# New tokens' values and outputs between rows and columns: DMA transfers of single elements through memory in place of PE transposes, in a RetNet/HGRN2 decoder step

## The chip, the cores and the metric

The kernel runs on one core of one Trainium2 chip. The metric is the device time of one launch in microseconds (us). All times of the trace come from one profiled execution and are counted from the start of its span.

The engines are named as the profile names them: PE (matrix multiply; PEld is its weight load), DVE (vector), ACT (scalar and activation), POOL, and SP, which only issues DMAs here. A name with q (SPq) is an engine's instruction queue. DMAs can also be issued from ACT and POOL; they stand in that engine's own order of instructions.

## The reference

One decoder layer for 512 prompt tokens and 8 new tokens, of width 1024, in fp32. After a norm, one wide product gives the inputs of two branches.

```python
z = h @ w_in                                   # rq rk rv rg gq gf gi gg a_ret a_hg
o_r, s_ret = retention_chunked(q_r, k_r, v_r, log_gamma, s_ret0)     # 4 heads, 128 x 256 states
u_r = head_norm_gate(o_r, ret_norm_g, rg) @ w_up_ret
o_g, s_hg = gla_chunked(q_g, k_g, v_g, log_f, s_hg0)                 # 8 heads, 128 x 128 states
u_g = head_norm_gate(o_g, hg_norm_g, gg) @ w_up_hg
m = sigmoid(a_ret) * u_r + sigmoid(a_hg) * u_g
r = r + m @ w_o
r = r + square(relu(rms_norm(r) @ w_ff1)) @ w_ff2
r = r + sigmoid(rms_norm(r) @ w_ple_gate) * (p_l @ w_ple_proj)
```

The change concerns the 8 new tokens of both branches. For each token `b` and head, with its own state `S`:

```python
S = decay * S + outer(k, v)      # decay: one number per head (retention) or one per key channel (HGRN2)
o = q @ S                        # then normed over the head's values and gated
```

The outputs are the layer's results for the prompt and the new tokens and all updated states.

## The kernel before

**Layout.** Activations lie by channel: 128 channels on the partitions, the `N = 520` tokens (512 prompt, 8 new) along the free dimension, in `T:N` the new ones. A product with 128 columns of weights is a *unit*: its weights `raw` are loaded by SP (`load`, L142; 128 rows of a weight's 128 columns per partition, 8 blocks), cut into a high and a low part (`prep`, L199: ACT writes `wh` at L221, DVE `wl` at L226), and multiplied in three passes of 8 blocks and two halves of the tokens (`mm`, L239: 48 matmuls at L243). The result is in one of two pairs of psum banks (`pm`); an evacuation by ACT or DVE takes it out. Other matmuls and transposes use four single banks (`bank`).

**Order.** `run_unit` (L269) writes the order out by hand: prepare the weights of a unit two ahead (and issue a load), the first half of the unit's matmuls, then all functions listed in `at[u]`, then the second half, then the evacuation. Engines run their own instructions in that order. The HGRN2 branch has 8 units per pair of heads, for four pairs; retention has 12 units per two heads, twice (L828 to L852). With `b` the first unit of a pair, the HGRN2 steps for new tokens are:

- `b+4` `hg_dec_load` (states loaded as `Sd`, key channels on the partitions), `b+7` `hg_dec_decay` and `hg_vT`,
- `hg_vT` (L468) calls `v_dec` (L453): the 8 new tokens' values, by channel in `vT[:, z, T:N]`, are transposed by PE (L457) into 8 rows of psum, copied by DVE into `vd` (L458) and stored by SP as an 8 x 256 tensor `vdd` in memory (L460). `v_bc` (L463) then loads `vdd` with every row on all partitions, as `vbc`.
- `b+9` and `b+11` `hg_dec_add`: DVE multiplies `vbc` by `k` (L486), adds it to `Sd` (L487), and SP stores the new state.
- `b+12` `hg_dec_out` (L511) calls `o_dec` (L493): four matmuls (L499) of the last 32 tokens' `q` with the state give a 128 x 512 psum block, in which only the rows 24 to 31 of each group of 32 are new tokens, and of each of these rows only the columns of the token's own state count. ACT copies the block to `psd` (L501).
- `b+13` `hg_state` (L528) ends with `o_ext` (L503): four PE transposes of the whole block (L506) and one DVE copy of the entries that count into `odec` (L509), by channel.
- `b+14` `hg_out`: ACT and DVE read `odec` (L565, L568). `b+15` `hg_norm`: `ones_bc` (L584) sums the squares over channels on PE (L590, L591).

Retention, with `o` the first unit of a head's turn (`o` of the second head of two is four units later):

- `o+6` `rt_vT` (L706): loads of `rSd`, PE transposes and ACT copies of the prompt's values (L722), then `v_dec` and two `v_bc`.
- `o+8`, `o+9` `rt_dec_add`: POOL multiplies `vbc` (L755), DVE adds (L756).
- `o+10` `rt_dec_out` (L762): `o_dec`, with `rt["knp"][:, 1]` (in the profile `rkn`) as the block. At the first head of two, `rt_kT` and `rt_vT` of the second head stand in the same unit, behind it.
- `o+11` `rt_ext` (L795), in the middle of the unit: `o_ext`, then the readers of `odec` (ACT L800, DVE L801), the sum of the two squares (DVE L802) and its cut into `rsqH` (ACT L598, DVE L599).
- `o+12` `rt_norm` (L808), in the middle of the unit: `ones_bc` on `rsqH` (PE L590, L591). For the last head it is at the same distance (L1010).

The rest of the layer (the up projections and gates, w_o, the MLP, the gated embedding) follows after about 480 us and is not touched.

Of the kernel before, what the change touches and what calls it, by code (L numbers as in the profile page):

```python
# [8 lines left out]
F32 = mybir.dt.float32  # L9
# [8 lines left out]
T = 512  # L18
NB = 8
N = T + NB  # L20
# [25 lines left out]
def decoder_step_kernel(  # L46
# [27 lines left out]
    V, S, G, PE = nc.vector, nc.scalar, nc.gpsimd, nc.tensor  # L74
    dma = nc.sync.dma_start
# [7 lines left out]
    dp = ctx.enter_context(tc.tile_pool(name="dp", bufs=2, space=DRAM))  # L83
# [11 lines left out]
    vd = cp.tile([8, 256], F32, name="vd")  # L95
    odec = cp.tile([128, 2, 8], F32, name="odec")

    ident = cid[:, C_ID:C_ID + 128]
# [9 lines left out]
    def pair(tag, name, dt=F32):  # L108
        return big.tile([128, 2, N], dt, tag=tag, name=name)

    def bank():
        return pss.tile([128, 512], F32, tag="s", name="s")
# [2 lines left out]
        return ap.rearrange("p (a n) -> p a n", a=2)  # L115

    units = []
    at = defaultdict(list)
    extra = set()
    prep_last = set()  # L120

# [109 lines left out]
    def prep_all():  # L231
        for _ in prep():
            pass
# [5 lines left out]
    def mm(w, k, xh, xl, ps, first, last):  # L239
        wh, wl = w  # L240
        for i, (a, b) in enumerate(((wh, xh), (wh, xl), (wl, xh))):
            for z in range(2):
                PE.matmul(ps[z], lhsT=a[:, k, :], rhs=b[:, z * NH:(z + 1) * NH],  # L243
                          start=first and i == 0, stop=last and i == 2)
# [3 lines left out]
    def run_groups(u, lo, hi):  # L248

        due = []  # L250
        n = 0
        for gi, (slots, start, stop, evac) in enumerate(units[u].groups):
            for si, (k, xs) in enumerate(slots):
                if lo <= n < hi:
                    if si == 0 and start:
                        if gi < 2:
                            t = pm.tile([128, 2, 512], F32, tag="m", name="m")
                            psum_of["cur"] = t[:, :, :NH], [t[:, z, :NH] for z in range(2)]
                        else:
                            psum_of["cur"] = None, [bank()[:, :NH] for z in range(2)]  # L260
                    both, ps = psum_of["cur"]
                    xh, xl = xs()
                    mm(w_of[u], k, xh, xl, ps, start and si == 0, stop and si == len(slots) - 1)
                    if si == len(slots) - 1 and evac is not None:
                        due.append((evac, both if both is not None else ps))
                n += 1
        return due

    def run_unit(u):  # L269
        prep_all()  # L270
        if u in extra:
            prep_all()
        due = run_groups(u, 0, 4)
        for f in at.pop(u, []):
            f()
        for e, ps in due:
            e(ps)
        for e, ps in run_groups(u, 4, 8):
            e(ps)
        w_of.pop(u)  # L280

    def unit(w, c, H, L, evac):
        units.append(Unit(cols(w, c), [([(k, lambda k=k: (H(k), L(k))) for k in range(8)], True, True, evac)]))
# [16 lines left out]
    st = {}  # L300
# [151 lines left out]

    def v_dec(vT):  # L453

        b = bank()
        for z in range(2):
            PE.transpose(b[0:8, z * 128:(z + 1) * 128], vT[:, z, T:N], ident)  # L457
        V.tensor_copy(vd, b[0:8, 0:256])  # L458
        d = dp.tile([8, 256], F32, tag="vd", name="vdd")
        dma(d, vd)  # L460
        return d

    def v_bc(d, z, tag):  # L463
# [29 lines left out]
    def o_dec(q, Sd, psd):  # L493

        b = bank()
        for g in (1, 0):
            for z in range(2):
                i = 2 * g + z
                PE.matmul(b[32 * i:32 * i + 32, :], lhsT=q[g],  # L499
                          rhs=Sd[g][:, 4 * z:4 * z + 4, :], start=True, stop=True)  # L500
        S.activation(psd, b, AF.Copy)  # L501

    def o_ext(psd):  # L503
        b = bank()
        for l in range(4):
            PE.transpose(b[:, l * 128:(l + 1) * 128], psd[:, l * 128:(l + 1) * 128], ident)  # L506

        own = bass.AP(b.tensor, b.offset + 24, [list(b.ap[0]), [64, 2], [36, 2], [129, 4]])
        V.tensor_copy(odec.rearrange("p g (z l) -> p g z l", z=2), own)  # L509

    def hg_dec_out(p):  # L511
        def go():
            q = st["q", p]
            o_dec([q[:, h, N - 32:N] for h in range(2)], [st["Sd", h] for h in range(2)], st["psd"])
        return go

    def hg_kT(p):
# [10 lines left out]
    def hg_state(p):  # L528
        def go():
            kn, vn, tot = st["kn"], st["vn"], st["tot"]  # L530
            Sst = big.tile([128, 2, 4, 128], F32, tag="S11", name="Sst")
            bs = []
            for h in range(2):
                b = bank()
                for c in range(4):
                    PE.matmul(b[:, c * 128:(c + 1) * 128], lhsT=kn[:, h, c, :], rhs=vn[:, h, c, :],  # L536
                              start=True, stop=True)
                bs.append(b)
            for h in range(2):
                V.tensor_copy(Sst[:, h, 0, :], bs[h][:, 0:128])  # L540
            for c in range(1, 4):
                for h in range(2):
                    i = TOFF[128] + c
                    V.scalar_tensor_tensor(Sst[:, h, c, :], in0=Sst[:, h, c - 1, :], scalar=tot[:, h, i:i + 1],
                                           in1=bs[h][:, c * 128:(c + 1) * 128], op0=ALU.mult, op1=ALU.add)
            st["S"] = Sst
            o_ext(st["psd"])
        return go

    def hg_out(p):  # L550
# [46 lines left out]
    def split(H, L, x):  # L597
        S.activation(H, x, AF.Copy)  # L598
        V.tensor_sub(L, x, H)  # L599
# [23 lines left out]
    for p in range(4):  # L623
        b = len(units)
# [22 lines left out]
    rt = {}  # L647
# [48 lines left out]
    def rt_kT(P, e):  # L696
        def go():
            hd = 2 * P + e
            K = rt["K", P][:, e]
            b = bank()  # L700
            for c in range(4):
                PE.transpose(b[:, c * 128:(c + 1) * 128], K[:, c * 128:(c + 1) * 128], ident)
            S.activation(rt["knp"][:, 0, 0:512], b, AF.Copy, scale=cst[:, C_KD + hd:C_KD + hd + 1])
        return go
# [57 lines left out]
    def rt_dec_out(P, e):  # L762
        def go():
            q = rt["Q", P][:, e, N - 32:N]
            o_dec([q, q], [rt["Sd", 0], rt["Sd", 1]], rt["knp"][:, 1, 0:512])
        return go

    def rt_out(P, e):
# [25 lines left out]

    def rt_ext(P, e):  # L795
        def go():
            o_ext(rt["knp"][:, 1, 0:512])
            sq, t = rt["sq"], rt["t"]
            for z in range(2):
                S.activation(sq[:, z, T:N], odec[:, z], AF.Square)  # L800
                V.tensor_tensor(t[:, z, T:N], t[:, z, T:N], odec[:, z], op=ALU.mult)  # L801
            V.tensor_tensor(sq[:, 0], sq[:, 0], sq[:, 1], op=ALU.add)  # L802
            hd = 2 * P + e
            rt["sqH"] = pair(OSLOT[hd], "rsqH", F32R)
            split(rt["sqH"][:, 0], rt["sqH"][:, 1], sq[:, 0])
        return go
# [21 lines left out]
    for P in range(2):  # L828
        b = len(units)
        for e in range(2):  # L830
            unit(W, RK + (2 * P + e) * 128, hk, hl, ev_rope(P, e, "K", KSCALE))
        for e in range(2):
            unit(W, RQ + (2 * P + e) * 128, hk, hl, ev_rope(P, e, "Q", 1.0))
        for e in range(2):
            for base, ev in ((RV, ev_rv), (RG, ev_rg)):
                for z in range(2):
                    unit(W, base + (2 * P + e) * 256 + z * 128, hk, hl, ev(P, e, z))
        for e in range(2):
            o = b + 4 * e
            at[o + 5].append(rt_scores(P, e))  # L840
            at[o + 6].append(rt_kT(P, e))
            at[o + 6].append(rt_vT(P, e))
            at[o + 7].append(rt_state(P, e))
            at[o + 8].append(rt_dec_add(P, e, 0))
            at[o + 9].append(rt_dec_add(P, e, 1))
            at[o + 10].append(rt_dec_out(P, e))
            at[o + 11].append(rt_ext(P, e))
            if P == 0 or e == 0:
                at[o + 12].append(rt_norm(P, e))
                at[o + 12].append(rt_scale(P, e))  # L850
        for e in range(2):
            at[b + 4 * e + 8].append(rt_out(P, e))  # L852
# [568 lines left out]
    for c in range(4):  # L1421
        t = big.tile([128, D], F32, tag=f"S{12 + c}", name=f"xn{c}")
# [172 lines left out]
    for u in flow[2:]:  # L1595
        if isinstance(u, int):
            run_unit(u)
        else:
            run_pair(*u)
# [68 lines left out]
```

## Time and profile before

| | us |
|---|---|
| median of 3 runs | 1088.88 |
| the three runs | 1087.69, 1088.88, 1089.11 |
| the profiled execution | 1087.63 |
| its span | 1085.8 |

TensorE's mean granted clock in the profiled execution is 0.999. The span is what the engines' instructions cover; the execution's own time is 1.83 us longer. In a timeline row stand the start, the length, the engine, the line, the operation and `output<-input`, with `x` and the number of instructions merged into the row, and in brackets the time for which the engine was idle before it and what it waited for. The length of a matmul includes its way through the array; matmuls in a row overlap. Names in the profile are those of the program's tiles: `vT` and `rvT` are the values by channel, `cid` holds the identity, `s` is any single psum bank, `m` a pair of them.

### The profile page before, as it was taken

The page shows a single profiled execution, that of the slowest core. Times are in us where ns is not written, and L with a number is a line of the kernel's source. Part 1 is how long each engine was busy: PE and PEld are TensorE (multiplying, and loading weights), DVE is VectorE, ACT ScalarE, POOL GpSimd, SP SyncE. Part 2 cuts the span into 40 slices and gives each one's busy share as a digit, 9 for nine tenths or more (in the row PEclk, how much of TensorE's full clock was granted, in tenths as well). Part 3 has the DMA queues.
Part 4 walks back from the last instruction along what each step waited for, and adds up shares of the span by engine and source line. Part 5 has one row for each costly group of instructions (what it writes and reads, how often), then busy time and mean ns, then how long its engine had stood idle before and what let it go on. Part 6 is the DMA issues. An engine that isn't in the chain of part 4 may idle for free.

```text
span 1085.8 us, 23533 instructions
## 1 busy us (share of the span) xinstructions
PE 1074.4 (99%) x10197; PEld 1057.2 (97%) x10197; DVE 686.2 (63%) x1074; ACT 508.6 (47%) x853; POOL 103.8 (10%) x95
## 2 busy tenths in 40 slices
PE   8999999999999999999999999999999999999997
PEld 8999999999999999999999999999999999999997
DVE  6576676858754844775666656855555555554565
ACT  7323534334254333554444345545455445544556
POOL 1000000000011010112222000011211211100001
PEclk9999999999999999999999999999999999999999
DMA  7556253442456355437778532355566566544302
GB/s 224 156 178 176 84 150 91 137 123 86 130 162 177 105 156 169 134 96 174 187 179 189 149 98 81 95 123 150 142 151 156 148 155 145 137 117 117 98 20 80
DMA packets 234952, 147.23 MB, mean 136 GB/s; under 512 B 5320, under 2 KB 229840, under 8 KB 234592
## 3 DMA queue, kind: packets, MB, share of 16 engines
q1 hardware_dynamic: 211600, 125.54, 39.1%
q0 software_dynamic: 23104, 19.93, 10.4%
q8 instruction: 80, 1.31, 0.5%
q14 instruction: 24, 0.20, 0.1%
q10 hardware_dynamic: 144, 0.26, 0.1%
HBM read 131.94 MB, written 13.76 MB: 134 GB/s over the span
## 4 chain that ended last, share of the span: by engine, by line
PE 95%; DVE 3%; ACT 1%; DMA 0%; issue 0%; SPq 0%; DVEq 0%
PE m L243 61%; PE s L881 19%; PE m L1394 2%; PE s L1394 2%; PE s L380 1%; PE s L499 1%; PE s L785 1%; PE s L560 1%; PE s L536 1%; PE s L739 1%; PE s L243 1%; PE s L562 0%; PE s L787 0%; DVE wl L226 0%; DVE tmp L659 0%; PE s L363 0%
## 5 line engine op out<-in xcount | busy, mean ns | idle before, releaser
L226 DVE TENSOR_TENSOR wl<-raw,wh 128x1024 fp32r<-128x1024 f32 (+1 forms) x125 | 152.3, 1220 | 69.2 <-ACT wh L221 68.2
L243 PE MATMUL m<-hH,wh 128*128 128x260 f32 x864 | 179.1, 289 | 0.0
L243 PE MATMUL m<-hH,wl 128*128 128x260 f32 x864 | 174.4, 283 | 0.0
L243 PE MATMUL m<-hL,wh 128*128 128x260 f32 x864 | 173.7, 283 | 0.0
L221 ACT ACTIVATE wh<-raw 128x1024 fp32r<-128x1024 f32 (+1 forms) x125 | 130.6, 1047 | 79.8 <-PE m L243 61.9
L243 PEld LDWEIGHTS m<-hH,wh 128*128 128x128 f32 x864 | 132.9, 189 | 2.5 <-issue 0.8
L243 PEld LDWEIGHTS m<-hL,wh 128*128 128x128 f32 x864 | 133.1, 188 | 0.0
L243 PEld LDWEIGHTS m<-hH,wl 128*128 128x128 f32 x864 | 133.1, 188 | 0.0
L881 PE MATMUL s<-comb,wh 128*128 128x260 f32 x672 | 122.1, 282 | 0.0
L881 PEld LDWEIGHTS s<-comb,wh 128*128 128x128 f32 x672 | 103.8, 188 | 0.0
L881 PE MATMUL s<-comb,wl 128*128 128x260 f32 x336 | 95.1, 283 | 0.0
L173 ACT ACTIVATE wh<-cst 128x512 fp32r<-128x512 f32 x80 | 50.3, 628 | 52.7 <-DVE cst L179 27.7
L175 DVE TENSOR_TENSOR wl<-cst,wh 128x512 fp32r<-128x512 f32 x80 | 55.2, 690 | 29.0 <-ACT wh L173 28.4
L243 PE MATMUL m<-fa,wh 128*128 128x260 f32 x384 | 66.9, 283 | 0.0
L243 PE MATMUL m<-oga,wh 128*128 128x260 f32 x384 | 64.6, 283 | 0.0
L881 PEld LDWEIGHTS s<-comb,wl 128*128 128x128 f32 x336 | 63.2, 188 | 0.0
L755 POOL TENSOR_TENSOR vbc<-vbc,K 128x1024 f32<-128x1024 f32 x8 | 17.5, 2198 | 409.4 <-ACT sq L580 298.1
L243 PEld LDWEIGHTS m<-fa,wh 128*128 128x128 f32 x384 | 54.7, 188 | 0.0
L243 PEld LDWEIGHTS m<-oga,wh 128*128 128x128 f32 x384 | 53.7, 188 | 0.8 <-issue 0.8
L1104 DVE TENSOR_TENSOR xT<-xT,m 128x520 f32<-128x520 f32 x32 | 22.3, 696 | 48.4 <-PE m L243 48.4
L243 PE MATMUL m<-fh,wh 128*128 128x260 f32 x256 | 51.5, 282 | 0.0
L243 PE MATMUL m<-fa,wl 128*128 128x260 f32 x256 | 51.5, 283 | 0.0
(396 smaller groups left out, 2438.4 us busy)
## 6 DMA issues: line engine op xcount, KB each, us to landing
raw<-in_w_in_dram SPq DMA_DIRECT2D x56, 512.0 KB, 4.2
raw<-in_w_ff_dram SPq DMA_DIRECT2D x40, 512.0 KB, 4.0
cst<-in_w_ff_dram POOLq DMA_DIRECT2D x48, 256.0 KB, 4.9
rawp<-in_w_ff_dram SPq DMA_DIRECT2D x24, 512.0 KB, 3.6
vbc<-vdd SPq DMA_DIRECT2D x16, 512.0 KB, 4.3
rawp<-in_w_in_dram SPq DMA_DIRECT2D x16, 512.0 KB, 3.4
cst<-in_w_in_dram POOLq DMA_DIRECT2D x28, 256.0 KB, 4.9
Sd<-in_state_hgrn_dram SPq DMA_DIRECT2D x8, 512.0 KB, 5.9
```

The source lines that it names most:

```text
L173: S.activation(wh[:, 4 * h:4 * h + 4], x, AF.Copy)
L175: V.tensor_sub(wl[:, 4 * h:4 * h + 4], x, wh[:, 4 * h:4 * h + 4])
L221: S.activation(wh[:, k], r[:, k], AF.Copy)
L226: e1.tensor_sub(wl[:, k], r[:, k], wh[:, k])
L243: PE.matmul(ps[z], lhsT=a[:, k, :], rhs=b[:, z * NH:(z + 1) * NH], start=first and i == 0, stop=last and i == 2)
L380: PE.matmul(b[32 * j:32 * j + 32, 32 * hc:32 * hc + 32], lhsT=kx[:, h, o:o + 32], rhs=qx[:, h, o:o + 32], start=True, stop=True)
L499: PE.matmul(b[32 * i:32 * i + 32, :], lhsT=q[g], rhs=Sd[g][:, 4 * z:4 * z + 4, :], start=True, stop=True)
L536: PE.matmul(b[:, c * 128:(c + 1) * 128], lhsT=kn[:, h, c, :], rhs=vn[:, h, c, :], start=True, stop=True)
L755: G.tensor_tensor(t, t, rt["K", P][:, e, T:N].unsqueeze(2).to_broadcast([128, 8, 128]), op=ALU.mult)
L881: PE.matmul(out, lhsT=w[:, 4 * half + k, :], rhs=x, start=start and k == 0 and m == 0, stop=k == 3 and m == 2, skip_group_check=not start)
L1104: V.tensor_tensor(h2(xT[:, j]), h2(xT[:, j]), ps, op=ALU.add)
L1394: PE.matmul(ps, lhsT=w[:, k, :], rhs=x, start=k == 0 and n == 0, stop=k == 7 and n == 2)
```

## The change

`v_dec` no longer uses PE, DVE and `vd`: ACT issues two DMAs, each of which writes the 128 channels x 8 tokens of a half of `vT[:, :, T:N]` to `vdd` element by element, with rows and columns exchanged. `o_ext` is replaced by two functions. `o_park` stores the whole 128 x 512 block in memory (`pd`), by a DMA that ACT issues directly behind its copy of the block. `o_fetch` reads the 16 entries per channel that count into `odec`, by four DMAs on SP of 128 x 4 single elements.

For HGRN2, `o_park` stands in `hg_dec_out` (`b+12`) and `o_fetch` where `o_ext` stood (`hg_state`, `b+13`). For retention both stand in `rt_dec_out` (`o+10`). `rt_ext` moves from the middle of unit `o+11` to the end of its matmuls, ahead of its evacuation, by a second list `before_end`.

```diff
@@ run_unit
-        for e, ps in run_groups(u, 4, 8):
+        due = run_groups(u, 4, 8)
+        for f in before_end.pop(u, []):
+            f()
+        for e, ps in due:
             e(ps)
@@ v_dec
-        b = bank()
+        d = dp.tile([8, 256], F32, tag="vd", name="vdd")
         for z in range(2):
-            PE.transpose(b[0:8, z * 128:(z + 1) * 128], vT[:, z, T:N], ident)
-        V.tensor_copy(vd, b[0:8, 0:256])
-        d = dp.tile([8, 256], F32, tag="vd", name="vdd")
-        dma(d, vd)
+            S.dma_start(d[:, z * 128:(z + 1) * 128].rearrange("t v -> v t"), vT[:, z, T:N])
         return d
@@ o_ext becomes o_park and o_fetch
-    def o_ext(psd):
-        b = bank()
-        for l in range(4):
-            PE.transpose(b[:, l * 128:(l + 1) * 128], psd[:, l * 128:(l + 1) * 128], ident)
-
-        own = bass.AP(b.tensor, b.offset + 24, [list(b.ap[0]), [64, 2], [36, 2], [129, 4]])
-        V.tensor_copy(odec.rearrange("p g (z l) -> p g z l", z=2), own)
+    def o_park(psd):
+
+        st["pd"] = dp.tile([128, 512], F32, tag="pd", name="pd")
+        S.dma_start(st["pd"], psd)
+
+    def o_fetch():
+        pd = st["pd"]
+        for i in range(4):
+            g, z = divmod(i, 2)
+            own = bass.AP(pd.tensor, pd.offset + (24 + 64 * g + 36 * z) * 512, [[1, 128], [640, 4]])
+            dma(odec[:, g, 4 * z:4 * z + 4], own)
@@ hg_dec_out
             o_dec([q[:, h, N - 32:N] for h in range(2)], [st["Sd", h] for h in range(2)], st["psd"])
+            o_park(st["psd"])
@@ hg_state
-            o_ext(st["psd"])
+            o_fetch()
@@ rt_dec_out
             o_dec([q, q], [rt["Sd", 0], rt["Sd", 1]], rt["knp"][:, 1, 0:512])
+            o_park(rt["knp"][:, 1, 0:512])
+            o_fetch()
@@ rt_ext
-            o_ext(rt["knp"][:, 1, 0:512])
             sq, t = rt["sq"], rt["t"]
@@ the order of retention
-            at[o + 11].append(rt_ext(P, e))
+            before_end[o + 11].append(rt_ext(P, e))
```

More of the change, by code (lines that the diff above doesn't have):

```diff
@@ L117, in decoder_step_kernel @@
     units = []
-    at = defaultdict(list)
+    at, before_end = defaultdict(list), defaultdict(list)
     extra = set()
```

## The prediction

> **What bounds the kernel now.** The page comes first: busy time by engine, and the chain that ended last.
>
> ```profile
> PE 1074.4 (99%) x10197; PEld 1057.2 (97%) x10197; DVE 686.2 (63%) x1074; ACT 508.6 (47%) x853; POOL 103.8 (10%) x95
> ...
> PE 95%; DVE 3%; ACT 1%; DMA 0%; issue 0%; SPq 0%; DVEq 0%
> ```
>
> PE is busy 99% of the span and makes 95% of the chain. A busy PE need not be at its peak, so the view of who waited for whom, on PE alone, comes next (us in total, times, longest).
>
> ```profile
> PE m L1485 <- DMA xs<-in_x_sample_dram: 3.4, 1, 3.4
> PE s L499 <- DVE Sd L487: 0.9, 1, 0.9
> ...
> ```
>
> It has six rows; the four not shown are under 0.5 us each. The largest lies at the kernel's start. So time taken off PE's stream comes off the span, unless a new wait appears on PE. The question is whether eight times two detours through memory stay behind PE's other work.
>
> **What PE loses.** Each of the eight heads or pairs of heads that are worked on together (four HGRN2 pairs, four retention heads; a "site" below) has two transposes in v_dec (L457) and four in o_ext (L506): 48 in all. Matmuls overlap, so the length of one isn't its price; the step between starts is. PE's timeline in two retention sites (start, length, engine, line; x2 is two instructions merged):
>
> ```profile
> 336.17 0.38 PE L457 MATMUL s<-cid,rvT 128*8 128x128 f32 x2
> 336.31 0.48 PE L243 MATMUL m<-hH,wh 128*128 128x260 f32 x2
> 336.63 0.40 PE L243 MATMUL m<-hL,wh 128*128 128x260 f32 x2
> ...
> 372.20 0.61 PE L506 MATMUL s<-cid,rkn 128*128 128x128 f32 x4
> 372.56 0.49 PE L243 MATMUL m<-hH,wh 128*128 128x260 f32 x2
> 372.89 0.40 PE L243 MATMUL m<-hL,wh 128*128 128x260 f32 x2
> 373.12 0.40 PE L243 MATMUL m<-hH,wl 128*128 128x260 f32 x2
> ```
>
> An undisturbed pair of L243 steps by 0.23 to 0.24 us (372.89 to 373.12). From the first L506 to the second pair behind it is 0.69 us; less one pair, the four cost 0.45 us. From the first L457 to 336.63 is 0.46 us; less one pair, the two cost 0.22 us. Per site that is 0.67 us, for eight **5.4 us**. DVE also loses two copies per site and SP one store; PE waits for neither, so I cost them at nothing.
>
> **What a transfer of single elements costs.** The new v_dec issues, on ACT, two DMAs of 1024 elements of 4 bytes each. o_park stores 256 KB in whole rows. o_fetch issues, on SP, four DMAs of 512 single elements. No row shows a data packet of 4 bytes, so I bound it with these, from the page's DMA parts (packets, MB, share of 16 engines; then issues, KB each, median us to landing):
>
> ```profile
> q1 hardware_dynamic: 211600, 125.54, 39.1%
> ...
> q10 hardware_dynamic: 144, 0.26, 0.1%
> ...
> raw<-in_w_in_dram SPq DMA_DIRECT2D x56, 512.0 KB, 4.2
> ...
> rawp<-in_w_in_dram SPq DMA_DIRECT2D x16, 512.0 KB, 3.4
> ...
> out_dram<-y SPq DMA_DIRECT2D x3, 256.0 KB, 3.0
> ```
>
> q10 is one store of 256 KB, 128 rows of 2 KB, in 144 packets: one per contiguous run and sixteen more. By that rule raw (rows of 128 columns) has 1024 packets of 512 bytes, 64 per engine; rawp (rows of 256) has the same bytes in 512 packets, 32 per engine. It lands 0.8 us sooner, so 32 more packets cost about **25 ns each**: the price of a packet beyond its bytes, which I take for a packet of 4 bytes. The bounds: 0 below (the packets hidden in the fixed part), and 4.2 us over 64, 66 ns, above (raw's whole landing put on its packets). Between them stands the mean of q1: 39.1% of 16 x 1085.8 us over 211600 packets is 32 ns, bytes included.
>
> Both detours thus put 128 packets on each engine: v_dec 2 x 1024 / 16, o_fetch 4 x 512 / 16. At 25 ns that is 3.2 us, with the fixed part on top. SP's timeline prices that one: the broadcast waits for the store of vd, 8 rows.
>
> ```profile
> 67.58 0.30 SPq L460 DMA_DIRECT2D vdd<-vd  x1
> 68.94 0.38 SPq L465 DMA_DIRECT2D vbc<-vdd  x1
> ```
>
> So 1.4 us pass from an issue until the next DMA may read the result, and an issue itself takes 0.30 to 0.38 us.
>
> One rule of the Trainium skill speaks against the change: VectorE: DVE Perf Modes, section The three transpose paths, calls a plain DMA with transposing strides 19 times slower than the crossbar's transpose, for which it gives 1309 ns at 128x128. An estimate from that page: 24.9 us for 16384 elements, 1024 per engine, is 24 ns each, so that rule alone would leave the sum as it is. No run here shows it.
>
> **The values' way (v_dec).** Tightest are the HGRN2 sites after the first. ACT's timeline, then DVE's:
>
> ```profile
> 127.27 1.07 ACT L476 ACTIVATE vn<-s 128x512 f32<-128x512 f32 x2
> ```
>
> ```profile
> 142.02 1.22 DVE L486 TENSOR_TENSOR vbc<-vbc,kx 128x1024 f32<-128x1024 f32 x1
> ```
>
> ACT triggers from 128.3 to 129.1 (2 x 0.38). With 1.4 + 3.2 us the values lie in memory at 133.7; v_bc is issued and lands (0.4 us, and 4.2 us as raw, of its size) at 138.3. DVE wants it at 142.0, so 3.7 us are spare, which last to 53 ns a packet. On SP the weight loads (L237) queue behind the waiting v_bc. In the first site v_bc went at 68.94; now it goes near 70, and a weight is prepared two units ahead of its matmuls (48 matmuls, 24 pairs at 0.24 us, some 6 us a unit), so that does no harm. The triggers hold ACT about 0.8 us; behind them waits an evacuation whose psum buffer PE wants one unit later, and that covers it.
>
> **The outputs' way (o_park, o_fetch).** For HGRN2 there is room: the park is issued at hg_dec_out, the fetch one unit later on SP behind the weight load of 104.12, and its first reader runs at 115.44 on ACT.
>
> ```profile
> 104.12 9.57 SPq L237 DMA_DIRECT2D raw<-in_w_in_dram  x2
> ```
>
> ```profile
> 115.44 0.20 ACT L565 ACTIVATE sq<-odec 128x8 f32<-128x8 f32 x1
> ```
>
> 11.3 us less 1.4 + 3.2: 6.7 us spare. The retention heads decide. Heads 1 and 2 on ACT, on PE (the sums in rt_norm, which must not start late), and on DVE:
>
> ```profile
> 334.94 0.60 ACT L501 ACTIVATE rkn<-s 128x512 f32<-128x512 f32 x1 [2.38 <-PE s L499]
> ...
> 336.09 1.08 ACT L722 ACTIVATE rvn<-s 128x512 f32<-128x512 f32 x2
> ...
> 366.47 0.60 ACT L501 ACTIVATE rkn<-s 128x512 f32<-128x512 f32 x1 [3.10 <-PE s L499]
> ```
>
> ```profile
> 350.10 0.28 PE L590 MATMUL s<-rsqH,ones_r 128*128 128x260 f32 x1
> ...
> 378.40 0.28 PE L590 MATMUL s<-rsqH,ones_r 128*128 128x260 f32 x1
> ```
>
> ```profile
> 373.40 0.17 DVE L509 COPY odec<-s 128x16 f32<-128x16 f32 x1
> ...
> 375.36 0.70 DVE L599 TENSOR_TENSOR rsqH<-rsq,rsqH 128x520 fp32r<-128x520 f32 x1 [0.71 <-ACT rsqH L598]
> ```
>
> From odec present (373.57) to the last input of the sums (376.06) pass 2.5 us. **Head 2:** the park is triggered at 367.1 and lands 3.0 us later (as out_dram<-y, of its size), at 370.2 with the wait; the fetch has until 378.40 - 2.5 - 0.1 = 375.8. That leaves 5.6 us for 1.4 us and 128 packets: enough up to 33 ns each, 1.0 us spare at 25. **Head 1:** the fetch starts at 338.8 and is needed by 347.5, 8.7 us; but v_dec of the next head starts at 337.4 on ACT's queue, so 256 packets per engine share the time and are done at 338.8 + 256 x the price: enough up to 34 ns, 2.3 us spare at 25. Heads 3 and 4 repeat these two. Behind the park's trigger on ACT wait the copies L703 and L722, which PE reads a unit later. While DVE and ACT wait at rt_ext, the evacuation of that unit and the next weight preparation stand behind them; at 25 ns DVE resumes near 375 (370.2 + 4.6), against 373.4, and PE wants that psum buffer only for the unit after next. SP, held by the fetch until the park lands, has state and weight loads behind it, with more than a unit to spare.
>
> **Sum.** The profiled execution took 1087.63 us, 1.83 us more than its span; the median of the runs shown, 1088.88, is 1.25 us above it. 1087.63 - 5.4 = 1082.2 for such an execution, **1083.5 us** as a median, -0.5%.
>
> **Rivals.** Above 34 ns every further ns costs PE 2 x 0.128 + 2 x 0.256 = 0.77 us, so the gain of 5.4 us is gone at 41 ns.
> 1. *A wait on PE takes the transposes' place, about as long*: 37 to 44 ns, 1086.7 to 1091.1, some 1088.5 us. For it: q1's mean of 32 ns lies just below the limit. Against: that mean carries 593 bytes a packet.
> 2. *Slower, by the same mechanism*: the sums of rt_norm wait for o_fetch in all four retention heads, from 41 ns on. At the upper bound of 66 ns it is 32 x 0.77 - 5.4 = +19 us, 1108 us. For it: no row has so small a read or write of memory. Against: the slope of 25 ns from rawp to raw. The Trainium skill, DMA: Bandwidth & Descriptors, section Specifications, says that below 512 bytes the engines read, modify and write; if that doubled the 32 ns, an estimate of 64 ns would land here. No run here shows it.
> 3. *A weight load shares the engines with a fetch*: 64 packets at 32 ns, 2.0 us, of which 1.0 is spare in heads 2 and 4: +2, 1085.5 us. For it: weight loads run throughout. Against: the fetch stands ahead of the next one on SP.
>
> **How the numbers follow.** Forecast 0.50 (own range 1082.3 to 1086.5), rival 1 0.15, rival 2 0.25, rival 3 0.10. Faster by over 0.2% (2.2 us, about what a measurement of this kernel can tell from no change): 0.60; within: 0.15; slower: 0.25. The low end is the forecast less another 1.2 us, the wait of L499 (0.9) and a little more that an unloaded DVE may end. The high end is 53 ns, where the values' way fails too: 1083.5 + 19 x 0.77 = 1098. Beyond the two ends I leave 0.05 and 0.15.
>
> **What would show it.** No L457 and no L506, 48 matmuls fewer, and 8 x 4096 data packets of single elements more. v_dec's DMAs and the fetches landing near 4.6 us where they run alone. No wait of PE at L590 for rsqH, and rt_ext's readers of odec in heads 2 and 4 starting near 8 us after the end of L501. The prediction is wrong if such landings pass 6 us, if PE waits at L590 or for a psum buffer, or if DVE L486 waits for vbc.

## The result, and the profile after

| | before | after |
|---|---|---|
| median of 4 runs, us | 1088.36 | 1105.15 |
| lowest and highest, us | 1087.69, 1089.11 | 1100.73, 1107.81 |
| profiled execution, us | 1087.63 | 1107.81 |
| its span, us | 1085.8 | 1106.0 |
| mean granted clock | 0.999 | 0.992 |

The kernel is slower: the ratio is 1.0148, with a 95% interval from 1.0136 to 1.016. The forecast was 1083.5 us and the range ended at 1098.

The page of the changed kernel, with the rows that answer to those of before (busy time; two DMA queues; the chain that ended last):

```profile
PE 1079.9 (98%) x10149; PEld 1061.4 (96%) x10149; DVE 687.3 (62%) x1058; ACT 508.9 (46%) x853; POOL 105.5 (10%) x95
...
q1 hardware_dynamic: 228368, 125.54, 39.9%
...
q10 hardware_dynamic: 17936, 2.43, 1.9%
...
PE 90%; DVE 4%; DMA 3%; ACT 1%; issue 1%; SPq 0%; another core or an unknown queue 0%; DVEq 0%; ACTq 0%
```

PE executes the 48 instructions fewer, yet is busy 5.5 us longer, in a span that is 20.2 us longer. The single elements stand in the packet counts: 16768 more on q1 and 17792 more on q10. Their bytes are nothing. The view of waits, PE only (us in total, times, longest), tells where PE stood:

```profile
PE m L243 <- issue: 6.6, 6, 2.0
PE s L595 <- ACT rsqH L603: 4.7, 2, 3.0
PE m L1491 <- DMA xs<-in_x_sample_dram: 3.4, 1, 3.4
PE m L243 <- DVE rA L664: 3.1, 1, 3.1
PE s L596 <- DVE rsqH L604: 0.7, 2, 0.4
```

Three kinds of wait are new. L595 and L596 (L590 and L591 before) are the sums in `rt_norm`: two heads' outputs come late, the wait that rival 2 named. L664 is the evacuation by DVE that falls behind after the first of them, and not for that alone: L604 takes 1.72 us at 366.94 and L761 2.92 us at 368.58, beside two instructions of POOL that begin at 365.19; before, the same two (L599, L756) took 1.24 and 1.22. "issue" means that PE stands and waits for nothing that the profile shows; the prediction had no term for it. The rest is in the clock. Windows of the changed kernel (us; busy time and count of PE, PEld, DVE, ACT, POOL; granted clock; DMA share; GB/s):

```profile
200.00:204.00 4.00, 2.90 (x16) 2.79 (x16) 1.39 (x3) 0.00 (x0) 0.00 (x0) 0.66 0.10 23
204.00:208.00 4.00, 4.00 (x35) 3.87 (x36) 3.29 (x6) 1.56 (x2) 0.00 (x0) 0.91 0.85 243
```

```profile
370.00:380.00 10.00, 6.89 (x47) 6.57 (x49) 9.91 (x14) 1.06 (x1) 0.42 (x1) 0.83 0.41 120
380.00:450.00 70.00, 70.00 (x574) 67.78 (x567) 35.41 (x47) 24.69 (x35) 3.80 (x2) 1.00 0.65 130
450.00:465.00 15.00, 11.87 (x75) 11.36 (x74) 7.55 (x8) 9.05 (x15) 4.26 (x2) 0.77 0.89 211
```

In these three places, where PE has stood for 2 to 3 us, the clock falls: 0.17 x 10 + 0.23 x 15 is 5.2 us, and the 8 us from 200 on, around the longest "issue" wait, add 0.34 x 4 + 0.09 x 4 = 1.7. So the profiled execution's 20.2 us are: -5.4 for the transposes, +6.6 "issue" at L243 and +0.3 at L383, +4.7 and +0.7 for the sums, +3.1 for rA, +6.9 for the clock, and +1.2 because this execution starts its first L243 1.2 us later (27.90 against 26.66). The runs of the kernel before lie near 1087.7 or near 1088.9, which is the same step; only one of them has a trace. That makes 18.1 of 20.2. Most of the rest may lie in how a wait is counted, from the end of one matmul: in a row that end overlaps the next by 0.16 us (a pair of L243 is 0.40 long and steps by 0.24), which for the 12 new waits is an estimated 1.9 us.

What came late? ACT's and SP's timelines in the second HGRN2 site: the triggers of `v_dec`'s writes, and `v_bc`, which waits for them.

```profile
129.05 1.92 ACTq L460 DMA_DIRECT2D vdd<-vT  x2
```

```profile
139.32 0.36 SPq L465 DMA_DIRECT2D vbc<-vdd  x1
```

The working had 5.4 us from the first trigger to `v_bc` (133.7 against 128.3). It took 10.3. And the engines are not the reason. The last HGRN2 site triggers its writes at 256.68, its `v_bc` goes at 266.39; the windows from before and within:

```profile
255.80:260.00 4.20, 4.20 (x38) 4.20 (x37) 3.95 (x6) 3.80 (x6) 0.00 (x0) 1.00 0.56 98
260.00:266.40 6.40, 4.98 (x99) 4.78 (x99) 4.32 (x4) 2.17 (x3) 0.00 (x0) 1.00 0.00 0
```

For 6.4 us the DMA share is 0.00 and nothing moves, though the writes are not reported as done; SP, which would issue the next loads, stands at `v_bc` meanwhile. In the same stretch PE loses 1.4 us to "issue". The trace also records single packets: the 4-byte packets of this site's writes start between 257.59 and 259.93, with a median of 7 ns each, and the last ends at 259.94, 6.5 us before `v_bc`. So the engines carry the elements about as quickly as the prediction had it; the time passes between the last packet and the report that the writes are done.

Other transfers stand with them. Head 3 on ACT (park, then the writes of the next head's values) and on SP (the fetch):

```profile
437.35 0.34 ACTq L506 DMA_DIRECT2D pd<-rkn  x1
...
438.15 0.37 ACTq L460 DMA_DIRECT2D vdd<-rvT  x1
...
438.56 0.74 ACTq L460 DMA_DIRECT2D vdd<-rvT  x1
```

```profile
448.70 2.02 SPq L513 DMA_DIRECT2D odec<-pd  x4
```

The park of 256 KB, for which I had 3.0 us, took 11.35, though the last of its 128 packets of 2 KB ends at 440.85. Head 2, beside which no values are written, shows the same three steps undisturbed (ACT, then SP):

```profile
381.59 0.34 ACTq L506 DMA_DIRECT2D pd<-rkn  x1
...
387.99 0.21 ACT L806 ACTIVATE rsq<-odec 128x8 f32<-128x8 f32 x1 [0.83 <-DMA odec<-pd]
```

```profile
383.91 2.02 SPq L513 DMA_DIRECT2D odec<-pd  x4
```

2.3 us for the park (its last packet ends 0.55 us before the fetch), and 4.1 us from the fetch's issue to its last reader. The reads of single elements cost in sum what the working said; the writes do not.

### The profile page after: what moved, and what is told of

Same layout as the page of the kernel before. It is cut to its first block, busy times and chain, and to the rows that moved or that the text cites. A ratio compares the mean times of both kernels' runs of the same rounds, so it can differ in the third digit from the quotient of the medians.

```text
span 1106.0 us, 23513 instructions
## 1 busy us (share of the span) xinstructions
PE 1079.9 (98%) x10149; PEld 1061.4 (96%) x10149; DVE 687.3 (62%) x1058; ACT 508.9 (46%) x853; POOL 105.5 (10%) x95
## 4 chain that ended last, share of the span: by engine, by line
PE 90%; DVE 4%; DMA 3%; ACT 1%; issue 1%; SPq 0%; another core or an unknown queue 0%; DVEq 0%; ACTq 0%
PE m L243 56%; PE s L887 18%; PE m L1400 2%; PE s L1400 2%; DMA pd<-rkn 1%; DMA odec<-pd 1%; PE s L383 1%; PE s L499 1%; PE s L541 1%; PE s L565 1%; PE s L792 1%; DVE wl L226 1%; PE s L243 1%; PE s L567 0%; PE s L1475 0%
## 5 line engine op out<-in xcount | busy, mean ns | idle before, releaser
L243 PE MATMUL m<-hH,wh 128*128 128x260 f32 x864 | 180.7, 290 | 6.2 <-issue 3.1
L243 PE MATMUL m<-hL,wh 128*128 128x260 f32 x864 | 175.1, 284 | 2.0 <-issue 2.0
L243 PE MATMUL m<-hH,wl 128*128 128x260 f32 x864 | 175.4, 285 | 1.4 <-issue 1.4
L243 PEld LDWEIGHTS m<-hH,wh 128*128 128x128 f32 x864 | 134.2, 190 | 9.6 <-issue 8.0
L243 PEld LDWEIGHTS m<-hH,wl 128*128 128x128 f32 x864 | 134.3, 190 | 3.4 <-issue 3.4
L243 PEld LDWEIGHTS m<-hL,wh 128*128 128x128 f32 x864 | 134.3, 190 | 0.0
L243 PE MATMUL m<-fa,wh 128*128 128x260 f32 x384 | 66.9, 283 | 0.0
L243 PE MATMUL m<-oga,wh 128*128 128x260 f32 x384 | 64.5, 283 | 0.0
L243 PEld LDWEIGHTS m<-fa,wh 128*128 128x128 f32 x384 | 54.7, 188 | 0.0
L243 PEld LDWEIGHTS m<-oga,wh 128*128 128x128 f32 x384 | 53.7, 188 | 0.8 <-issue 0.8
L243 PE MATMUL m<-fh,wh 128*128 128x260 f32 x256 | 51.5, 282 | 0.0
L243 PE MATMUL m<-fa,wl 128*128 128x260 f32 x256 | 51.5, 283 | 0.0
```

## The experiments

Two theories stood at first. **W**: the element-wise writes of `v_dec` are what is late, and they hold up the rest. Its rival **F**: the element-wise reads of `o_fetch` are. The first four kernels part them. In the diffs `...` stands for lines left out, such as the tiles that an added transfer needs.

**The outputs' way alone.** The changed kernel with the old `v_dec`:

```diff
@@ v_dec
-        d = dp.tile([8, 256], F32, tag="vd", name="vdd")
+        b = bank()
         for z in range(2):
-            S.dma_start(d[:, z * 128:(z + 1) * 128].rearrange("t v -> v t"), vT[:, z, T:N])
+            PE.transpose(b[0:8, z * 128:(z + 1) * 128], vT[:, z, T:N], ident)
+        V.tensor_copy(vd, b[0:8, 0:256])
+        d = dp.tile([8, 256], F32, tag="vd", name="vdd")
+        dma(d, vd)
```

> The changed kernel with v_dec as it was (16 PE transposes, DVE copy, store by SP); the outputs still go by o_park and o_fetch. Theory W (the element-wise writes of v_dec are the cause: they land 8 to 10 us after their issue, and meanwhile the park, the fetch and PE's own supply of instructions stand still): no PE gaps put down to issue in the HGRN2 sites, o_fetch landing about 4 us after its issue in all four retention heads, PE waits under 1 us per head, time 1085 to 1087 us (32 transposes less, 3.6 us). Theory F (the element-wise reads of o_fetch are the cause, my rival 2): heads 1 and 3 still lose 6 to 7 us each, 1097 to 1100 us.

Measured: 1087.05 us (median of 10) against 1088.82, ratio 0.9986, interval 0.9977 to 0.9996. PE's waits in it:

```profile
PE m L243 <- DVE rA L667: 1.0, 1, 1.0
...
PE s L599 <- DVE rsqH L607: 0.3, 1, 0.3
```

No "issue", no wait of microseconds for the sums. W holds. In head 1, beside which no values are written element by element now, the park takes 2.65 us (335.12 to 337.77) and the fetch 5.2 until its last reader (342.94); in the changed kernel it was 4.7 and 9.5 (343.25, 347.91, 357.37). Of the 3.6 us for 32 transposes 1.8 arrive (by the interval, 0.4 to 2.5); where the rest went is read further below.

**The values' way alone.** The kernel before with the new `v_dec`:

```diff
@@ v_dec
-        b = bank()
-        for z in range(2):
-            PE.transpose(b[0:8, z * 128:(z + 1) * 128], vT[:, z, T:N], ident)
-        V.tensor_copy(vd, b[0:8, 0:256])
         d = dp.tile([8, 256], F32, tag="vd", name="vdd")
-        dma(d, vd)
+        for z in range(2):
+            S.dma_start(d[:, z * 128:(z + 1) * 128].rearrange("t v -> v t"), vT[:, z, T:N])
```

> The kernel before with only v_dec changed to element-wise writes; o_ext stays on PE and rt_ext in its old place. Theory W: PE gaps put down to issue of 1 to 2.5 us in each HGRN2 site, 9 to 10 us in all, less 1.8 us for 16 transposes; in the retention heads v_bc goes out some 12 us after the triggers and POOL and DVE may get late by a few us; 1096 to 1100 us. Theory F: 1086 to 1087 us.

Measured: 1097.97 us (median of 4, 1095.29 to 1106.53), ratio 1.0102, interval 1.0059 to 1.0146. PE's waits:

```profile
PE m L243 <- issue: 6.4, 6, 1.6
...
PE m L243 <- DVE rA L656: 0.7, 1, 0.7
PE s L380 <- issue: 0.6, 1, 0.6
```

The "issue" waits come with the writes alone. The trace is of the quickest of the four runs; the slowest, at 1106.53, has a granted clock of 0.990 against 0.998 and no trace. The two halves add up to +9.2 - 1.8 = +7.4 us; together they cost 16.8. The other 9.4 us (some 3 to 12, by this run's interval) would arise where both meet: the trace of the changed kernel has the sums, rA and most of the clock in and behind heads 1 and 3, whose park and fetch stand with the writes.

**The writes alone, for nobody.** The kernel before, with the same writes into memory that only a small transfer on POOL reads, to show when they are done; four HGRN2 sites:

```diff
...
+            x = dp.tile([8, 256], F32, tag="xd", name="xd")
+            for z in range(2):
+                S.dma_start(x[:, z * 128:(z + 1) * 128].rearrange("t v -> v t"), vT[:, z, T:N])
+            G.dma_start(rd, x[:, 120:136])
```

> The kernel before, and in each of the four HGRN2 sites the same two element-wise writes of v_dec in addition, into memory that no part of the computation reads; a DMA on POOL that reads a corner of it shows when they have landed. Theory W: they land 8 to 10 us after their issue and PE shows gaps put down to issue of 1 to 2.5 us per site although nothing waits for the data: 1094 to 1100 us. Theory F, or any theory by which only the waiting for data costs time: no PE gaps, 1088 to 1090 us.

Measured in a single run: 1097.52 us, 8.7 above the median before. Its ACT and POOL timelines in the first site, and PE's waits:

```profile
65.59 0.39 ACTq L482 DMA_DIRECT2D xd<-vT  x1
```

```profile
76.96 0.74 POOL L483 DMA_DIRECT2D rd<-xd  x1 [63.13 <-DMA xd<-vT]
```

```profile
PE m L244 <- issue: 5.0, 6, 2.1
...
PE s L381 <- issue: 1.6, 2, 1.0
```

11.4 us to completion, and PE stands for 6.6 us although no instruction of the kernel needs the data. So the waits of PE are not for late values; pending writes of this kind stop PE by another way. That this way is the supply of PE's instructions from memory is a guess that I did not test. The packets of the instruction queue (q8, 16 KB each) do not settle it: two of them, at 74.59 and 140.68, take 2.0 and 2.8 us beside pending writes, where the median is 1.1, but PE goes on at 201.73 and at 266.26, before that queue's next packets begin (202.33 and 267.84). POOL's small transfer is not the cause: it stands in the quick variants below too, without any "issue" wait.

**The reads alone, for nobody.** The mirror of it, two DMAs on SP that read 2 x 1024 single elements of `vdd` to 128 partitions:

```diff
...
+            for z in range(2):
+                dma(rdT[:, z], st["vd"][:, z * 128:(z + 1) * 128].rearrange("t v -> v t"))
+            G.tensor_copy(rdC, rdT)
```

> The kernel before, and in each HGRN2 site the mirror image of these transfers in addition: vdd is read back element by element (2 x 1024 packets of 4 bytes, from memory to 128 partitions), issued on SP behind v_bc; only a small copy on POOL waits for it. Theory W: it lands 3 to 5 us behind v_bc, no PE gaps, 1087.5 to 1089.5 us. A rival to W, that any 2048 packets of 4 bytes stall the other transfers whichever way they go: PE gaps as in d1, 1094 to 1100 us.

Measured in a single run: 1088.96 us, within the runs of before (1087.63 to 1089.02), and no "issue" wait. On SP and POOL:

```profile
70.59 1.58 SPq L483 DMA_DIRECT2D rdT<-vdd  x2
```

```profile
76.89 1.21 POOL L484 COPY rdC<-rdT 128x16 f32<-128x16 f32 x1 [63.29 <-DMA rdT<-vdd]
```

6.3 us from the first issue, behind a `v_bc` of 512 KB on the same queue. Reads of this shape are harmless to PE.

**What makes the writes slow?** The 2048 elements go to 8 KB, sixteen to 64 bytes. One theory (T1) was that elements from different partitions, carried by several engines, meet in one 64-byte stretch; another (T2) that every write of a few bytes is slow, wherever it goes. Three variants of the writes for nobody change only where the elements go; only the two lines that differ are shown.

```diff
@@ each channel's eight elements in 64 bytes of their own, 8 bytes apart, 16 KB
+            x = dp.tile([256, 8, 2], F32, tag="xd", name="xd")
+                S.dma_start(x[z * 128:(z + 1) * 128, :, 0], vT[:, z, T:N])
@@ every element 64 bytes from the next, 128 KB
+            x = dp.tile([8, 256, 16], F32, tag="xd", name="xd")
+                S.dma_start(x[:, z * 128:(z + 1) * 128, 0].rearrange("t v -> v t"), vT[:, z, T:N])
@@ a channel's eight elements as one row of 32 bytes
+            x = dp.tile([256, 8], F32, tag="xd", name="xd")
+                S.dma_start(x[z * 128:(z + 1) * 128, :], vT[:, z, T:N])
```

> As the run with unread writes, but each channel's 8 elements go to a stretch of 64 bytes of their own, 8 bytes apart: again 2 x 1024 packets of 4 bytes into 16 KB, but no two channels, and so no two of the engines that share the channels, write into one stretch. Theory T1 (it is several engines writing into the same short stretch of memory that is slow): lands 2 to 5 us after its issue, no PE gaps, 1088 to 1090 us. Theory T2 (every write of a few bytes to memory is slow, wherever it goes): lands 8 to 11 us after, PE gaps of 1 to 2.5 us per HGRN2 site, 1094 to 1099 us.

> As the run with unread writes, in the same order, but all elements 64 bytes apart: 2 x 1024 packets of 4 bytes spread over 128 KB, no two into the same 64 bytes. T1: lands 2 to 5 us after its issue, no PE gaps, 1088 to 1090 us. T2: lands 8 to 11 us after, PE gaps, 1094 to 1099 us. If the size of the region matters (8 KB against 128 KB) the landing lies between.

> As the run with unread writes, but in whole rows of 8 tokens: 2 x 128 packets of 32 bytes, the same bytes into the same size of region. T1 and T2 alike: an eighth of the packets, lands 2 to 3 us after its issue, no PE gaps, 1088 to 1089.5 us. If it were the bytes or the region and not the number of writes, it would land as late as the 4-byte writes.

And one more, later: packed as in the change, but with the eight rows 16 KB apart.

```diff
+            x = dp.tile([8, 4096], F32, tag="xd", name="xd")
+                S.dma_start(x[:, z * 128:(z + 1) * 128].rearrange("t v -> v t"), vT[:, z, T:N])
```

> As the run with unread writes, packed as in the change, but the 8 tokens' rows stand 16 KB apart: the region spans 115 KB, nearly that of the writes 64 bytes apart, while 16 elements still share each 64 bytes. If it is the sharing of short stretches that is slow: lands 9 to 13 us after the first issue, PE gaps put down to issue, 1093 to 1098 us. If it is the small region: lands near 5 us after, no PE gaps, 1087.5 to 1089 us.

Measured, a single run of each. The completion is POOL's start less the first trigger on ACT, in the four HGRN2 sites:

| where the elements go | completion, us | time, us | runs before beside it | "issue" waits of PE |
|---|---|---|---|---|
| packed, rows 1 KB apart (as the change) | 11.4, 12.3, 12.9, 12.6 | 1097.52 | 1088.82 | 6.6 |
| 64 bytes of its own per channel | 12.1, 10.9, 10.4, 10.7 | 1093.22 | 1087.80 | 2.5 |
| every element 64 bytes apart, rows 16 KB apart | 6.1, 4.9, 4.9, 5.4 | 1087.56 | 1087.80 | none |
| rows of 32 bytes, one packet each | 4.7, 3.5, 3.6, 3.6 | 1088.76 | 1087.80 | none |
| packed, rows 16 KB apart | 35.3, 39.3, 47.4, 41.8 | 1201.59 | 1088.80 | 64.3 |

The rows behind two of these lines, the spread one and the worst, on ACT and on POOL:

```profile
125.92 1.00 ACTq L482 DMA_DIRECT2D xd<-vT  x2
```

```profile
130.86 0.63 POOL L483 DMA_DIRECT2D rd<-xd  x1 [59.65 <-DMA xd<-vT]
```

```profile
239.38 2.01 ACTq L482 DMA_DIRECT2D xd<-vT  x2
```

```profile
286.79 0.52 POOL L483 DMA_DIRECT2D rd<-xd  x1 [97.49 <-DMA xd<-vT]
```

The same 2048 elements, in packets of 4 bytes, take 4.9 or 47.4 us. So it is neither the number of packets nor their size, and T2 falls. Nor is it the pace of the engines: in both rows nine of ten packets start within 2.6 us of the first, with a median of 7 ns. T1 in its strict form falls too: with 64 bytes per channel, written from one partition only, completion is still 10 to 12 us. What the three slow variants share is that several elements go to the same 64 bytes one after another; 64 bytes is the only stretch tried, and two rows of 32 bytes share such a stretch without harm, in an eighth of the packets. The distance of the rows decides too, by a factor of three to four between the first line and the last, where 9 to 13 us had been expected, but not alone: the spread variant has the same 16 KB from row to row and is quick. Which rule of the memory's addresses stands behind it stays open.

**A repair for the values.** Rows of 32 bytes are quick to write, and reads were harmless; so ACT stores rows at the evacuation, and SP reads them element by element to the 8 partitions of `vd`, which it stores as before.

```diff
+    def v_rows(vT):
+        r = dp.tile([256, 8], F32, tag="vr", name="vr")
+        for z in range(2):
+            S.dma_start(r[z * 128:(z + 1) * 128, :], vT[:, z, T:N])
+        st["vr"] = r
@@ v_dec
+        dma(vd, st["vr"].rearrange("v t -> t v"))
...
-        for z in range(2):
-            S.dma_start(d[:, z * 128:(z + 1) * 128].rearrange("t v -> v t"), vT[:, z, T:N])
+        dma(d, vd)
```

> The changed kernel with the values' detour turned round, so that the element-wise half is a read: ACT stores the new tokens' values as 256 rows of 32 bytes right after they are evacuated, and where v_dec stood SP reads them element by element into vd (8 partitions), stores vd and goes on as before the change. All 48 transposes stay away. If only element-wise writes are harmful: no PE gaps put down to issue, PE waits at the sums of heads 1 to 4 as in the run with the values on PE (some 1.8 us in all), 5.4 - 1.8 = 3.6 us less than before, 1084 to 1086.5 us. If reads on eight partitions are slower than on 128, or SP is held too long, DVE waits for vbc and the time is 1088 us or more.

Measured: 1094.47 us (median of 5), ratio 1.0066, interval 1.0052 to 1.008: a miss; what came is the last case of the text above. SP's and PE's waits:

```profile
SPq L469 <- DMA vd<-vr: 60.1, 8, 8.9
```

```profile
PE m L243 <- DVE rA L673: 3.9, 1, 3.9
...
PE s L604 <- ACT rsqH L612: 1.8, 1, 1.8
...
PE s L508 <- DVE rSd L772: 1.3, 1, 1.3
```

The "issue" waits are gone, so they belong to the writes. But SP stands 7.5 us on average for the read, in which the 2048 elements go to 8 partitions by one DMA, where 2048 to 128 partitions by four took 4.1 us in head 2 of the changed kernel. I had carried the price of the one to the other; which of their differences makes it was not tested. `v_bc` and what follows on SP are late by it.

**Only where there is room.** The old `v_dec`; the outputs through memory in the HGRN2 sites and in heads 1 and 3, by PE at the old place in heads 2 and 4:

```diff
...
@@ rt_dec_out
-            o_park(rt["knp"][:, 1, 0:512])
-            o_fetch()
+            if e == 0:
+                o_park(rt["knp"][:, 1, 0:512])
+                o_fetch()
@@ rt_ext
+            if e == 1:
+                o_ext(rt["knp"][:, 1, 0:512])
...
```

> A version meant to beat both: values by PE as before the change; the outputs by o_park and o_fetch in the HGRN2 sites and in heads 1 and 3, where 8.7 us and more stand between the park and the need; heads 2 and 4, where the run with the values on PE still lost some 1.8 us to waits, keep o_ext and the old place of rt_ext. 24 transposes less, 24 x 0.1125 = 2.7 us, no new wait: 1085.5 to 1086.8 us, ratio 0.9975. If the waits in heads 2 and 4 are not what the run with the values on PE lost, it is no faster than that one, 1087 us.

Measured: 1086.97 us (median of 11) against 1088.80, ratio 0.9985, interval 0.9976 to 0.9994. That is 0.15% less than before, as with the outputs' way in all sites; 24 transposes gone are 2.7 us, and 1.8 are measured (by the interval, 0.6 to 2.6).

**Where a part of this gain goes** is read in the kernel with the outputs' way alone, where PE waits 1.0 us for rA near 362 us. SP issues the store of `vd` and `v_bc` behind the fetch there, which itself waits for the park; SP's timelines of this kernel and of before:

```profile
347.80 0.99 SPq L468 DMA_DIRECT2D vbc<-vdd  x2
```

```profile
342.56 0.99 SPq L465 DMA_DIRECT2D vbc<-vdd  x2
```

So POOL multiplies `vbc` later. POOL's and DVE's timelines:

```profile
351.88 1.90 POOL L763 TENSOR_TENSOR vbc<-vbc,K 128x1024 f32<-128x1024 f32 x1 [35.89 <-DMA vbc<-vdd]
354.01 2.62 POOL L763 TENSOR_TENSOR vbc<-vbc,K 128x1024 f32<-128x1024 f32 x1 [0.24 <-DMA vbc<-vdd]
```

```profile
352.47 2.40 DVE L831 TENSOR_TENSOR rt<-rt,rsq 128x1040 f32<-128x1040 f32 x1 [3.16 <-ACT rsq L590]
356.01 1.72 DVE L607 TENSOR_TENSOR ogb<-rt,orH 128x1040 fp32r<-128x1040 f32 x1 [1.14 <-ACT orH L606]
```

And before, where POOL had done its two by 351.97, on DVE:

```profile
353.37 1.24 DVE L822 TENSOR_TENSOR rt<-rt,rsq 128x1040 f32<-128x1040 f32 x1 [3.16 <-ACT rsq L582]
```

Two instructions of DVE that need 1.24 us take 2.40 and 1.72: 1.6 us more. The evacuation to rA begins at 361.07 there, at 360.34 before, and PE, which is earlier by its lost transposes, waits for it. The 1.16 us more of the first are about what POOL's instruction had still to run when it began (353.78 - 352.47 = 1.31), the 0.48 of the second too (356.63 - 356.01 = 0.62). The Trainium skill, SBUF — State Buffer, section SBUF: two separate sides, says that GpSimd and VectorE share a pair of ports, which the one that starts first locks for its whole instruction while the other waits, for VectorE also where it reads two inputs from SBUF, as here; the rows agree. The kernel with room shows a wait of 0.69 us for rA at the same place. Laid beside the trace of before, matmul by matmul, and leaving aside that its first L243 starts 1.25 us later, PE in the kernel with the outputs' way alone gains 0.33 to 0.55 us at each of the eight places of `o_ext`, 3.4 us in all, and loses 1.2 us at this wait for rA and 0.7 at the sums of head 4 (L599). The kernel with room does not lose the 0.7, but keeps 8 transposes more, which cost about as much. No run was made that moves POOL's work away, so that rA waits for POOL is read from the trace, not tested.

## Why the prediction was wrong

The step that failed is the sum under "What a transfer of single elements costs": 1.4 + 3.2 us until the data may be used, for read and write alike, with 25 ns a packet, bounded by 66 ns, worked out from loads of long rows. For the writes it was 10.3 us. As far as the packet records show, the part that was mis-sized is the 1.4, taken from a store of 8 rows, more than the 3.2; and PE's standing while such writes pend was put at nothing.

- **Reads.** Right as a sum: 4.6 us expected, 4.1 us in head 2 of the changed kernel. Its parts are not shown: the four issues alone take 2.02 us, and a 4-byte packet is recorded with a median of 9 ns.
- **Writes.** 1.4 + 3.2 us expected, 10.3 measured: (10.3 - 1.4) / 128 is 70 ns a packet, above the upper bound. But it is no price per packet: the packets start within 2.3 us in the last HGRN2 site, an estimated 18 ns apart on each of the 16 engines (2.3 us over 130), then the engines lie idle for 6.5 us; and the same packets are done after 4.9 us at other addresses. None of the rows from which I bounded it was a write of less than a row, and I let reads stand for writes.
- **The values' way.** The 3.7 us of spare were used up: DVE L486 ran at 146.50 instead of 142.02. Yet PE hardly paid for that: its wait at L499 is 0.7 us, 0.9 before. What I had not thought of is that the writes cost PE time by merely pending, 6.6 us, as the writes for nobody showed.
- **The outputs' way.** In heads 2 and 4, to which I gave the least spare (1.0 us), the fetch came in time: PE stands for 0.35 us at L596 in head 4 and not at all at the sums of head 2. In heads 1 and 3, to which I gave 2.3 us of spare, PE waited 1.75 and 2.98 us at L595, because I let the writes share the engines with the fetch by number of packets, while in truth park and fetch stood with them: 11.35 us for the park of head 3, 4.7 for that of head 1 and 9.5 for its fetch.
- **The transposes.** Right as the size of what PE loses, 0.45 and 0.22 us a site. Of this 3.4 us arrive without the writes, as read above, and two waits take half of it back: 1.8 of 3.6 us are measured.
- **Rival 2** had the sign and the wait, the sums of `rt_norm`, but in two heads, not four, and not through the fetch's own packets; with the values' way taken back, nearly all of it was gone. Its 1108 us lie near the 1105.15 by luck: it gave all of the loss to the sums, and most of it lies in "issue", rA and the clock. **Rivals 1 and 3** did not come about. The range ended at 1098 because I carried it only to 53 ns; it had no term for PE standing without a partner in the profile, nor for the clock.
- **The two pages.** The 24 ns worked out from the Trainium skill, VectorE: DVE Perf Modes, section The three transpose paths, lie near what the reads took in sum, (4.1 - 1.4) / 128 = 21 ns, and not the writes' 70; the 19 times stand there for a large innermost stride at the destination, which here only the writes have. The 64 ns worked out from the rule of the Trainium skill, DMA: Bandwidth & Descriptors, section Specifications, that less than 512 bytes are read, modified and written, come near the 70 ns of the packed writes. But the writes 64 bytes apart, of 4 bytes as well, do not show that price, nor do the reads; here the address decides, not the size alone.

## What to carry to other kernels

Price reads and writes of single elements apart, and a write by where it goes and until it is reported as done, not until its packets have gone out: in these runs writes of 4 bytes, several to the same 64 bytes, took two to ten times as long as the same writes 64 bytes apart, while the DMA share showed idle engines, and other transfers and PE stood meanwhile. Whole rows out and single elements in did better here than single elements out, for the values too (1094.47 against 1105.15), but there it still lost to the transposes: the reading side is measured in its own shape. A saving on the bounding engine is worth only as much as the next engine lets through: look at what the moved transfer makes coincide.

## What the runs showed that I had not expected

- Writes that nobody reads stopped PE for 6.6 us ("issue"), and for 64.3 us with the rows 16 KB apart, while neither reads of the same size nor writes spread out stopped it at all. By which way is open.
- After a pause of PE of some 3 us the granted clock was 0.50 for more than 5 us. The row, behind the wait of 2.98 us at 454.36:

```profile
455.00:460.00 5.00, 4.91 (x23) 4.91 (x24) 1.99 (x4) 4.79 (x6) 0.54 (x1) 0.50 1.16 299
```

The Trainium skill, TensorE: Matmul & The Clock Gate, section Why this matters for your kernels, warns of gaps above about 3 us between matmuls; this row agrees. But shorter waits were followed by a fall too, 2.00 us at 200.58, while 2.13 us at 76.32 in the kernel with unread writes were not (clock 1.00 from 73 to 80): the length of one wait alone does not decide. The wait of 2.98 us cost more than twice its length, with 0.23 x 15 = 3.4 us of half speed behind it.
- 2048 single elements read by one DMA to 8 partitions took 7.5 us of SP's waiting on average, by four DMAs to 128 partitions 4.1 us.
